# An MLP that streams its weights from HBM: seven raw buffers instead of five, transfers issued ten chunks ahead, and the kept banks of the last block fetched in two parts

## The chip, the cores and the metric

The kernel runs on one core of one Trainium2 chip, in a single launch. The metric is the device time in microseconds (us), lower is better. The kernel before the change was timed three times; the numbers below give the median and the spread.

## The reference, cut to what matters

A decoder trunk of two layers on one sequence of 256 tokens, 2048 features, all in float32. Each layer is an attention mixer, an MLP and a gated per-layer embedding (called PLE below). The change lies in the MLP and touches the start of the PLE that follows it:

```python
for i in range(DEPTH):                               # DEPTH = 2, D_MODEL = 2048, D_FF = 8192, SEQ = 256
    ...                                              # attention mixer A (layer 0) or B (layer 1)
    hn = rmsnorm(h, mlp_norm_g[i])
    h = h + jnp.square(jax.nn.relu(hn @ mlp_w1[i])) @ mlp_w2[i]
    gate = jax.nn.sigmoid(rmsnorm(h, ple_norm_g[i]) @ ple_w_gate[i])
    h = h + (p[i] @ ple_w_proj[i]) * gate
return rmsnorm(h, final_norm_g)
```

## The kernel before, in words

**Chunks.** Every weight is read once, in chunks of 128 partitions x 1024 float32 (512 KB). A chunk passes through four stations. SP issues its DMA into a tile `raw` (L262, queue order is program order). ACT copies it to a rounded tile `whi` (L274). DVE subtracts and so makes the remainder `wlo` (L282). TensorE then forms three products for each pair of operands, high x high, low x high and high x low, each with 512 columns (L525 in the pair scheme below, L636 in the plain scheme). There are 5 `raw`, 6 `whi` and 5 `wlo` buffers. A `raw` buffer is free again when its `wlo` has been made.

**The order of the work.** All instructions are laid down by `Program.run` (L144), which walks through the list of chunks. At the step of chunk `at` it first issues loads up to chunk `at + 7` (DMA_AHEAD), stopping earlier when the `raw` buffer that comes next in turn has not yet had its `wlo` laid down; then copies and subtractions up to about three chunks ahead (SPLIT_AHEAD); then every running generator is advanced by one `yield` (this is how evacuations, transposes, norms and other side work are spread over the steps); then come the matmuls of chunk `at`. So a generator's place in the order is counted in chunk steps, and each engine and each DMA queue works through its part of that order without overtaking.

**The MLP.** `mlp` (L790) runs over four blocks of the hidden width (NFB = 4, `b`), each with four groups of up products (`q`) and four of down products. Pairs of groups are made with a seven-product scheme (`pair_major`, L492): a chunk step is of kind `q` (plain, 12 matmuls) or one of `a`, `b`, `t`, `u`, where `t` and `u` are sums of raw chunks that DVE makes (L564, L569, L570) and have no load of their own; the raw tiles of `a` and `b` are held until `u`'s `wlo`. The sums over the blocks are kept in DRAM: for `b < 3`, `down_kept` (L967) adds each block's banks to DRAM tiles `s` (four 128x512 halves, in two tiles for each pair of groups) and `y` by accumulating DMAs on the POOL queue (L896). The hidden activations are transposed through DRAM on the POOL queue as well (L225, L229).

**The last block.** For `b = 3` the pair of groups 0 and 1 is made by `down_last` (L986), the groups 2 and 3 by the plain scheme. `fetch_shared(0)` (L944) reads the kept `s` tiles of the first pair into tiles `xf`. When the seven-product sums of the last block are there, `sums` adds them (L992), joins them (`from_sums`, L932 to L935) and issues on POOL, in this order: two accumulating DMAs that add `y[0]` and `y[1]` (L997), the fetch of the second pair's two `s` tiles (L944), and the fetch of `y[2]` and `y[3]` (L948). Each is 512 KB. `finish_sums(2)` is started behind them; after three `yield`s it joins the second pair's sums on DVE, and later adds `y[2]` and `y[3]` (`with_y`, L951). The first pair's result is finished by `done` (L1010), transposed on DVE (L761), sent through DRAM on the SP queue (`dU`, written at L225 and read back at L229) and added to the residual `x` (L778); then come the squares and the normed copies for the PLE (L379, L303 on ACT, L385, L311 on DVE). The groups 2 and 3 follow the same way (L906). The PLE's first chunks are loaded while this goes on, and one small product with the sum of squares `acc` (L320) closes the norm.

**Pools.** Tiles that live only during the MLP are in a pool `z`. It is opened 12 chunks into the MLP and closed after the last down chunk. `raw`, `whi` and `wlo` are in a pool of the whole program.

Of the kernel before, what the change touches and what calls it, by code (L numbers as in the profile page):

```python
# [10 lines left out]
F32 = mybir.dt.float32  # L11
# [4 lines left out]
P = 128  # L16
# [12 lines left out]
NFB = 4  # L29
CH = 1024  # L30
# [3 lines left out]
DMA_AHEAD = 7  # L34
SPLIT_AHEAD = 3
RAW_BUFS, HI_BUFS, LO_BUFS = 5, 6, 5
HF_BUFS = 3
FORM_LATER = (7, 9)
MIXED = (2, 3, 5, 6)
MIXED_QK = (5, 6, 7)  # L40
# [19 lines left out]
def f32(ap):  # L60
    return ap.bitcast(F32)
# [13 lines left out]
class Part:  # L75
# [3 lines left out]
    def __init__(self, src=None, make=None, cols=None, held=0):  # L79
        self.src, self.make, self.cols, self.held = src, make, cols, held  # L80
# [9 lines left out]
class Program:  # L90
# [7 lines left out]

    def __init__(self):
        self.steps, self.active, self.waiting, self.after = [], [], [], []  # L100

    def op(self, fn):
        self.steps.append((None, fn))

    def chunk(self, src, fn):
        self.steps.append((src if isinstance(src, Part) else Part(src), fn))

    def collect(self, fn):
        kept, self.steps = self.steps, []
# [31 lines left out]
        except StopIteration:  # L141
            pass

    def run(self, load, copy, sub):  # L144
        srcs = [s for s, _ in self.steps if s is not None]
        raw, hi, lo = {}, {}, {}
        held = []
        loaded = at = copied = subbed = 0
        for src, fn in self.steps:
            if src is None:  # L150
                g = fn()
                if g is not None:
                    self.begin(g)
                continue
            starting = at < KT // 2
            if starting:
                self.advance()
            urgent = [g.gen for g in self.waiting if isinstance(g, Urgent)]
            self.waiting = [g for g in self.waiting if not isinstance(g, Urgent)]
            for g in urgent:  # L160
                next(g)
            ahead = max(0, min(SPLIT_AHEAD, at - KT // 2 + 2))
            while loaded < len(srcs) and loaded <= at + DMA_AHEAD:
                if srcs[loaded].make is None:
                    if len(held) >= RAW_BUFS and held[-RAW_BUFS] >= subbed:
                        break
                    raw[loaded] = load(loaded, srcs[loaded].src)
                    held.append(loaded + srcs[loaded].held)
                loaded += 1
            while copied < loaded and copied <= at + ahead + (ahead > 0):  # L170
                if srcs[copied].make is not None:
                    raw[copied] = srcs[copied].make(raw, copied)
                hi[copied] = copy(copied, raw[copied], srcs[copied].cols)
                copied += 1
            while subbed < copied and subbed <= at + ahead:
                lo[subbed] = sub(subbed, raw[subbed], hi[subbed], srcs[subbed].cols)
                subbed += 1
            for n in [n for n in raw if n + srcs[n].held < subbed]:
                del raw[n]
            if not starting:  # L180
                self.advance()
            self.active += urgent
            self.waiting += fn(hi.pop(at), lo.pop(at)) or []
            self.finish_tensor()
            at += 1
        self.until(lambda: not self.active and not self.waiting)
# [3 lines left out]
def kernel(ctx: ExitStack, tc: tile.TileContext, a: dict, out: bass.AP):  # L190
    nc = tc.nc
    ctx.enter_context(tc.manual_schedule())
    prog = Program()
# [6 lines left out]
    wpool = ctx.enter_context(tc.tile_pool(name="w", bufs=4))  # L200
# [3 lines left out]
    cur = {}  # L204
# [6 lines left out]
    def close_pool(key):  # L211
        cur.pop(key)
        cur.pop(key + "/es").close()
# [41 lines left out]
    def load_x(j, order="xTA"):  # L255
        nc.sync.dma_start(xp[j], a[order][:, j * 2 * T:(j + 1) * 2 * T])


    def load(n, src):
        t = wpool.tile([P, CH], F32, tag="raw", name="raw", bufs=RAW_BUFS)  # L260
        for c in pieces(n) if n == 0 else [slice(0, CH)]:
            nc.sync.dma_start(t[:, c], src[:, c])  # L262
        if n < KT // 2 - 1:
            load_x(n + 1)
        return t

    def pieces(n):

        return [slice(0, CH // 2), slice(CH // 2, CH)] if n < 2 else [slice(0, CH)]
# [520 lines left out]
    def mlp(layer, xg, norm, to, norm2, opening):  # L790
# [3 lines left out]

        y = [dpool.tile([P, D // 2], F32, tag=f"y{q}", name=f"y{q}", bufs=1) for q in range(4)]
        shared = {q: [dpool.tile([P, D // 2], F32, tag=f"s{q}{i}", name=f"s{q}{i}", bufs=1) for i in range(2)] for q in (0, 2)}
        hid = [[None] * 16 for _ in range(NFB)]
# [18 lines left out]
        def up(b, q, t, late=0):  # L818
# [19 lines left out]
            for n in range(2 if third_group(b, q) else 1):  # L838
                if n:
                    for _ in range(FORM_LATER[b > 0]):  # L840
                        yield
# [6 lines left out]
                yield  # L848
                f = cur["z"].tile([P, 2, 2 * T], F32R, tag="hf", name="hf", bufs=HF_BUFS)
                f5 = f.rearrange("p c (i a r) -> p c a i r", i=4, r=32)  # L850
# [65 lines left out]
        def chunks(w, b, q):  # L916
            return lambda c: a[w][layer * 128 + (b * 4 + q) * 8 + c]
# [4 lines left out]
        def downs(b, q):  # L922
            token_major(chunks("w2", b, q), hid[b], lambda *ps: down(b, q, *ps), whole=True)

        def all_forms(these):
            for c in these:
                yield from x_forms(2 * c, G_MLP + layer, forms)
                yield
# [10 lines left out]
        def fetch_shared(q):  # L939

            kept[q] = [cur["z"].tile([P, 2, 2 * T], F32R, tag="xf", name="xf", bufs=len(MIXED)) for _ in range(2)]
            kept[q] = [f32(t) for t in kept[q]]
            for i in range(2):
                nc.gpsimd.dma_start(kept[q][i], shared[q][i])  # L944
# [8 lines left out]
            merged.add(q + i)  # L953

        def finish_sums(q):
            for _ in range(3):
                yield
            from_sums(*kept[q])
            for i in range(2):
                for _ in range(2):  # L960
                    yield
                with_y(q, i)

        def turning_tile(n):
            return f32(cur["z"].tile([P, 2, 2 * T], F32R, tag="hf", name="hf", bufs=HF_BUFS).rearrange("p c n -> p (c n)"))

# [19 lines left out]
        def down_last(q):  # L986
            ts = []

            def sums(aux):
                for t, names in zip(kept[q], (("P1", "R6"), ("Q5", "Q7"))):  # L990
                    for j, n in enumerate(names):
                        nc.vector.tensor_add(t[:, j], aux[n], t[:, j])  # L992
                    yield
                from_sums(*kept[q])
                yield
                for i in range(2):
                    nc.gpsimd.dma_start(kept[q][i], y[q + i], accum_op=ALU.add)  # L997
                fetch_shared(2)
                fetch(2)
                fetch(3)  # L1000
                prog.waiting.append(finish_sums(2))
                for _ in range(4):
                    yield
                ts.extend(kept[q])

            def done(i, ps):
                while not ts:
                    yield
                t = ts[i]
                nc.vector.tensor_add(t, ps, t)  # L1010
                yield
                w = yield from turned(t, turning_tile if i else new, steps=3)
                add_turned(q + i, w)
                yield
                yield from in_pairs(normed, q + i)

            return sums, done

        def down_mixed(b, q):
            sums, done = down_kept(b, q) if b < NFB - 1 else down_last(q)  # L1020
            m = mixed_down(b, q)
            if (b, q) == (0, 0):
                order = [(i, c) for i in range(2) for c in (1, 2, 3)] + [(0,)] + [(i, c) for c in (4, 5) for i in range(2)]
            else:
                order = [(0, c) for c in (1, 2, 3)] + [(0,)] + [(1, c) for c in (1, 2, 3)]
                order += [(4,)] if third_group(b, q) else [(0, 5), (1, 5), (4,)]
            if third_group(b, q):
                order += [(0, 6), (1, 6), (5,), (0, 7), (1, 7)]
            else:
                order += [(i, c) for i in range(2) for c in (6, 7)]  # L1030
            pair_major(lambda i, c: a["w2"][layer * 128 + (b * 4 + q + i) * 8 + c], order, hid[b], turned_forms[b], sums, done,
                       {(0, 0): {13: [lambda: all_forms(MIXED[3:])]}, (NFB - 1, 0): {1: [lambda: fetch_shared(0)]}}.get((b, q)), (3, 1, 0, 2), urgent=b < NFB - 1)

        up_mixed(0, 2)
        for b in range(NFB):
# [4 lines left out]
                up_mixed(b + 1, 2)  # L1040
        downs(NFB - 1, 2)
        downs(NFB - 1, 3)
        prog.op(lambda: close_pool("z"))
        prog.op(lambda: open_pool("j"))
        prog.op(lambda: open_pool("R", side="right"))
# [945 lines left out]
    prog.op(lambda: open_pool("E"))  # L1991
    ple(1, p1, x_p1, n_p1, None, n_fin, True)

    prog.run(load, copy, sub)
    close_pool("E")
    close_pool("j")
    close_pool("h")
# [121 lines left out]
```

## Time and profile before

| | |
|---|---|
| median of 3 runs | 2407.78 us (2405.53 to 2411.17) |
| the profiled execution | 2413.49 us, of which the instructions span 2411.7 us |
| TensorE busy | 2392.0 us, 11159 matmuls |
| DVE busy | 2059.4 us |
| ACT busy | 1519.9 us |
| DMA queue of SP | 508.37 MB, 65.7% of 16 engines' span |
| DMA queue of POOL | 68.19 MB, 10.9% |

The profile is of one execution. Its lines name an engine, a line of the kernel and tiles (`out<-in`); a bracket behind a timeline row gives the idle time of the engine before that row and what ended it. PE is TensorE's matmul, PEld its weight load. A PE that shows as busy need not run at its full rate, so lost time is better read from the number of matmuls in a stretch. Times in rows are counted from the first instruction. In this execution the MLP of layer 0 takes its pair-scheme products from 507 us and ends near 1133 us; that of layer 1 runs from 1670 us to near 2300 us; the last blocks begin near 1047 and 2210 us.

### The profile page before, as it was taken

How to read it: one execution, taken by the hardware profiler on the slowest of the kernel's cores; microseconds unless marked ns; L12 is line 12 of the kernel's file. 1: busy time of each engine (PE TensorE's matmuls, PEld its weight loads, DVE VectorE, ACT ScalarE, POOL GpSimd, SP SyncE). 2: the span in 40 equal slices, each digit the busy share in tenths (PEclk: the TensorE clock that was granted, in tenths of full speed). 3: DMA queues.
4: the chain of work that ended last, by engine and by line, in shares of the span. 5: the costliest groups of instructions: out<-in, count | busy, mean ns of one | idle time of the engine just before them, and what ended most of it. 6: DMA issues, size and time to landing. Idle time of an engine off the chain costs nothing.

```text
span 2411.7 us, 32754 instructions
## 1 busy us (share of the span) xinstructions
PE 2392.0 (99%) x11159; PEld 1993.6 (83%) x11159; DVE 2059.4 (85%) x2926; ACT 1519.9 (63%) x2211; POOL 144.6 (6%) x246
## 2 busy tenths in 40 slices
PE   9999999999999999999999999999999999999998
PEld 8888888888888888877788889988888888888777
DVE  7978886788999999897777989867999899898886
ACT  7555555666666656664564788756666666666466
POOL 0000000001001100111000000000100100111000
PEclk9999999999999999999999999999999999999999
DMA  8778678778778788889887853477868878878984
GB/s 287 238 233 264 222 246 284 233 220 269 236 258 257 247 259 253 252 264 283 252 241 205 266 158 123 136 231 220 281 216 259 262 250 244 258 246 274 267 269 148
DMA packets 181289, 579.44 MB, mean 240 GB/s; under 512 B 21633, under 2 KB 44161, under 8 KB 181121
## 3 DMA queue, kind: packets, MB, share of 16 engines
q1 hardware_dynamic: 160080, 508.37, 65.7%
q0 software_dynamic: 20464, 68.19, 10.9%
q8 instruction: 87, 1.43, 0.2%
q10 hardware_dynamic: 576, 0.79, 0.1%
q14 instruction: 82, 0.66, 0.1%
HBM read 511.21 MB, written 66.06 MB: 239 GB/s over the span
## 4 chain that ended last, share of the span: by engine, by line
PE 89%; DMA 4%; DVE 3%; issue 2%; ACT 1%; SPq 0%; POOL 0%; DVEq 0%; ACTq 0%; POOLq 0%
PE at L525 42%; PE at L636 15%; PE mm L525 10%; PE mm L636 10%; PE mm L415 4%; PE mm L417 2%; DVE wlo L282 1%; PE at L415 1%; DMA dU<-z 1%; DMA w<-dU 1%; DMA xf<-s 1%; PE at L417 1%; DMA raw<-in_w_proj 1%; PE at L1941 1%; DMA raw<-in_w 0%
## 5 line engine op out<-in xcount | busy, mean ns | idle before, releaser
L282 DVE TENSOR_TENSOR wlo<-raw,whi 128x1024 fp32r<-128x1024 f32 (+1 forms) x973 | 1103.2, 1161 | 205.0 <-ACT whi L274 67.7
L274 ACT CAST whi<-raw 128x1024 fp32r<-128x1024 f32 (+1 forms) x973 | 946.1, 1005 | 422.9 <-DMA raw<-in_w 117.1
L525 PE MATMUL at<-whi,xa 128*128 128x512 f32 x1512 | 465.9, 389 | 0.0
L525 PE MATMUL at<-whi,h 128*128 128x512 f32 x1408 | 433.5, 389 | 0.0
L525 PEld LDWEIGHTS at<-whi,xa 128*128 128x128 f32 x1512 | 283.7, 188 | 59.4
L525 PEld LDWEIGHTS at<-whi,h 128*128 128x128 f32 x1408 | 264.3, 188 | 54.7
L525 PE MATMUL at<-wlo,xa 128*128 128x512 f32 x756 | 294.2, 389 | 0.0
L636 PE MATMUL at<-whi,xa 128*128 128x512 f32 x928 | 287.4, 391 | 0.1
L525 PE MATMUL at<-wlo,h 128*128 128x512 f32 x704 | 274.3, 390 | 0.8 <-DVE wlo L282 0.8
L274 ACT CAST whi<-ts 128x1024 fp32r<-128x1024 f32 x98 | 103.3, 1054 | 186.8 <-DVE ts L564 149.1
L636 PE MATMUL mm<-whi,xa 128*128 128x512 f32 x656 | 204.1, 392 | 0.0
L636 PEld LDWEIGHTS at<-whi,xa 128*128 128x128 f32 x928 | 172.6, 188 | 36.1 <-ACT whi L274 0.8
L636 PE MATMUL at<-wlo,xa 128*128 128x512 f32 x464 | 180.9, 391 | 0.6 <-DVE wlo L282 0.6
L525 PEld LDWEIGHTS at<-wlo,xa 128*128 128x128 f32 x756 | 141.9, 188 | 29.6
L525 PEld LDWEIGHTS at<-wlo,h 128*128 128x128 f32 x704 | 132.1, 188 | 29.7 <-DVE wlo L282 2.4
L636 PEld LDWEIGHTS mm<-whi,xa 128*128 128x128 f32 x656 | 123.2, 189 | 25.0
L636 PE MATMUL mm<-wlo,xa 128*128 128x512 f32 x328 | 128.4, 391 | 2.3 <-DVE wlo L282 2.3
L564 DVE TENSOR_TENSOR ts<-raw 128x1024 f32<-128x1024 f32 x98 | 119.3, 1217 | 5.7 <-DMA raw<-in_w 4.6
L282 DVE TENSOR_TENSOR wlo<-ts,whi 128x1024 fp32r<-128x1024 f32 x98 | 119.4, 1219 | 2.5 <-PE at L636 1.6
L415 PE MATMUL mm<-xa,whi 128*128 128x512 f32 x336 | 109.8, 399 | 0.0
L636 PEld LDWEIGHTS at<-wlo,xa 128*128 128x128 f32 x464 | 87.1, 188 | 20.6 <-DVE wlo L282 2.3
L525 PE MATMUL mm<-whi,xf 128*128 128x512 f32 x324 | 99.9, 390 | 0.0
(443 smaller groups left out, 3487.3 us busy)
## 6 DMA issues: line engine op xcount, KB each, us to landing
raw<-in_w SPq DMA_DIRECT2D x512, 512.0 KB, 4.9
raw<-in_w_qk SPq DMA_DIRECT2D x96, 512.0 KB, 5.0
raw<-in_w_gate SPq DMA_DIRECT2D x64, 512.0 KB, 4.9
raw<-in_w_kv SPq DMA_DIRECT2D x48, 512.0 KB, 4.4
raw<-in_w_v SPq DMA_DIRECT2D x47, 512.0 KB, 5.3
raw<-in_w_q SPq DMA_DIRECT2D x32, 512.0 KB, 4.2
raw<-in_w_oB SPq DMA_DIRECT2D x32, 512.0 KB, 3.8
dU<-z POOLq DMA_DIRECT2D x30, 512.0 KB, 4.6
```

What stands on the lines that cost most here:

```text
L274: nc.scalar.copy(hi[:, c], t[:, c])
L282: nc.vector.tensor_sub(lo[:, c], t[:, c], f32(hi)[:, c])
L415: nc.tensor.matmul(ps, hi[:, col:col + P], rhs, start=first, stop=False)
L417: nc.tensor.matmul(ps[:, :T], lo[:, col:col + P], rhs[:, :T], start=False, stop=last)
L525: nc.tensor.matmul(ps, x_, w_, start=b not in touched, stop=end and last[b] == n and i == 2)
L564: nc.vector.tensor_add(halves(t), halves(a), b[:, None, :512].to_broadcast([P, 2, 512]))
L636: nc.tensor.matmul(st[j], *parts[j][i], start=k == i == 0, stop=k == kt - 1 and i == 2)
L1941: nc.tensor.transpose(tr[:, i * P:(i + 1) * P], src, ident)
```

## The change

It has two parts.

Seven raw buffers: while the MLP's chunks are loaded and `z` is open, loads go in turn to the five `raw` buffers and to two new buffers `rawx` in `z`, and the limit on how far ahead loads are issued goes from 7 to 10 chunks. The load that comes next still waits until the buffer it takes has had its `wlo` laid down. Chunks of other stages keep five buffers and the limit of 7.

The fetch in two parts: in the last block the fetch of the second pair's `s` tiles is taken out of `sums` and put behind step 14 of the pair's 20 steps (counted from 0), ahead of the accumulating DMAs; `finish_sums(2)` is started behind step 15. It now waits six `yield`s ahead of `from_sums`, then three and two ahead of the two `with_y`. The fetch of `y[2]` and `y[3]` stays where it was.

```diff
+RAW_MORE, MORE_AHEAD = 2, 3
...
     def chunk(self, src, fn):
-        self.steps.append((src if isinstance(src, Part) else Part(src), fn))
+        part = src if isinstance(src, Part) else Part(src)
+        part.deep = self.deep
+        self.steps.append((part, fn))
...
-        held = []
+        held, turn = {"raw": [], "more": []}, 0
...
-            while loaded < len(srcs) and loaded <= at + DMA_AHEAD:
+            while loaded < len(srcs):
+                more = srcs[loaded].deep and roomy()
+                if loaded > at + DMA_AHEAD + (MORE_AHEAD if more else 0):
+                    break
                 if srcs[loaded].make is None:
-                    if len(held) >= RAW_BUFS and held[-RAW_BUFS] >= subbed:
+                    turn = (turn + 1) % (RAW_BUFS + RAW_MORE) if more else 0
+                    tag, bufs = ("more", RAW_MORE) if turn > RAW_BUFS else ("raw", RAW_BUFS)
+                    if more and turn == 0:
+                        tag, bufs = "more", RAW_MORE
+                    if len(held[tag]) >= bufs and held[tag][-bufs] >= subbed:
+                        turn -= 1
                         break
-                    raw[loaded] = load(loaded, srcs[loaded].src)
-                    held.append(loaded + srcs[loaded].held)
+                    raw[loaded] = load(loaded, srcs[loaded].src, tag == "more")
+                    held[tag].append(loaded + srcs[loaded].held)
                 loaded += 1
...
-    def load(n, src):
-        t = wpool.tile([P, CH], F32, tag="raw", name="raw", bufs=RAW_BUFS)
+    def load(n, src, more=False):
+        t = cur["z"].tile([P, CH], F32, tag="rawx", name="rawx", bufs=RAW_MORE) if more else \
+            wpool.tile([P, CH], F32, tag="raw", name="raw", bufs=RAW_BUFS)
...
         def finish_sums(q):
-            for _ in range(3):
+            for _ in range(6):
                 yield
             from_sums(*kept[q])
             for i in range(2):
-                for _ in range(2):
+                for _ in range(3 - i):
                     yield
                 with_y(q, i)
...
                     nc.gpsimd.dma_start(kept[q][i], y[q + i], accum_op=ALU.add)
-                fetch_shared(2)
                 fetch(2)
                 fetch(3)
-                prog.waiting.append(finish_sums(2))
...
-                       {(0, 0): {13: [lambda: all_forms(MIXED[3:])]}, (NFB - 1, 0): {1: [lambda: fetch_shared(0)]}}.get((b, q)), (3, 1, 0, 2), urgent=b < NFB - 1)
+                       {(0, 0): {13: [lambda: all_forms(MIXED[3:])]}, (NFB - 1, 0): {1: [lambda: fetch_shared(0)], 
+                                         14: [lambda: fetch_shared(2)],
+                                         15: [lambda: finish_sums(2)]}}.get((b, q)), (3, 1, 0, 2), urgent=b < NFB - 1)
...
-    prog.run(load, copy, sub)
+    prog.run(load, copy, sub, lambda: "z" in cur)
```

More of the change, by code (lines that the diff above doesn't have):

```diff
@@ L100, in __init__ @@
         self.steps, self.active, self.waiting, self.after = [], [], [], []
+        self.deep = False
     def op(self, fn):
@@ L142, in begin, with run @@
             pass
-    def run(self, load, copy, sub):
+    def run(self, load, copy, sub, roomy):
         srcs = [s for s, _ in self.steps if s is not None]
         raw, hi, lo = {}, {}, {}
-        held = []
+        held, turn = {"raw": [], "more": []}, 0
         loaded = at = copied = subbed = 0
@@ L790, in mlp @@
     def mlp(layer, xg, norm, to, norm2, opening):
+        prog.deep = True
         y = [dpool.tile([P, D // 2], F32, tag=f"y{q}", name=f"y{q}", bufs=1) for q in range(4)]
@@ L1042, in mlp @@
         downs(NFB - 1, 3)
+        prog.deep = False
         prog.op(lambda: close_pool("z"))
```

## The prediction

> **What bounds the kernel now.** I read the page first, then the stretches table, then who ends TensorE's waits, then the timelines of DVE, ACT, POOL and SP around the last block of the MLP.
>
> ```profile
> PE 2392.0 (99%) x11159; PEld 1993.6 (83%) x11159; DVE 2059.4 (85%) x2926; ACT 1519.9 (63%) x2211; POOL 144.6 (6%) x246
> PE 89%; DMA 4%; DVE 3%; issue 2%; ACT 1%; SPq 0%; POOL 0%; DVEq 0%; ACTq 0%; POOLq 0%
> ```
>
> TensorE is busy for 99% of the span and carries 89% of the chain. The change takes no matmul away, so all it can win is time in which TensorE waits. The stretches table (stretch, length, then busy time and count of each engine, granted clock, DMA share, GB/s) says how much that is:
>
> ```profile
> 507.00:858.00 351.00, 351.00 (x1550) 290.66 (x1549) 322.80 (x366) 228.94 (x270) 38.86 (x66) 1.00 0.81 253
> 858.00:1047.00 189.00, 187.96 (x825) 153.97 (x824) 173.32 (x186) 121.03 (x139) 18.13 (x28) 1.00 0.82 251
> 1047.00:1135.00 88.00, 86.78 (x379) 70.59 (x378) 72.29 (x80) 42.62 (x50) 13.13 (x24) 1.00 0.91 283
> 1135.00:1167.00 32.00, 30.14 (x132) 24.28 (x132) 26.43 (x44) 23.35 (x43) 5.45 (x10) 1.00 0.82 255
> 1167.00:1180.00 13.00, 11.43 (x46) 9.07 (x45) 9.03 (x15) 5.87 (x8) 0.00 (x0) 0.87 0.77 252
> 2020.00:2210.00 190.00, 189.30 (x832) 155.46 (x831) 175.36 (x188) 122.64 (x141) 18.12 (x28) 1.00 0.82 250
> 2210.00:2300.00 90.00, 88.66 (x389) 72.53 (x388) 74.58 (x86) 44.90 (x56) 10.59 (x18) 1.00 0.93 281
> 2300.00:2329.00 29.00, 28.13 (x123) 22.60 (x122) 24.45 (x39) 21.43 (x36) 0.00 (x0) 1.00 0.79 263
> ```
>
> In 507 to 858 us TensorE never waits: 351.00 / 1550 = 0.2265 us per matmul. At that pace 825 matmuls take 186.8 us, so 858 to 1047 loses 2.2 us. In the same way 1047 to 1135 (last block, layer 0) loses 88 - 85.8 = 2.2, 1135 to 1167 (start of the PLE) 32 - 29.9 = 2.1; in layer 1, 2020 to 2210 loses 190 - 188.4 = 1.6, 2210 to 2300 loses 90 - 88.1 = 1.9, and 2300 to 2329 loses 29 - 27.9 = 1.1. The sum is 11.1 us. The stretch from 1167 holds 42 large matmuls (9.5 us) and four with one column, taken as 0.3 us together, so 3.2 us are lost there to something else: the last product of the norm (L320).
>
> What ends these waits, in the table of waits for TensorE's weight loads from 1047 to 1180 us (total, times, longest):
>
> ```profile
> PEld mm L636 <- DVE wlo L282: 2.8, 2, 2.1
> PEld at L636 <- DVE wlo L282: 2.0, 3, 0.8
> PEld mm L320 <- DVE acc L311: 2.0, 1, 2.0
> PEld at L525 <- DVE wlo L282: 0.8, 1, 0.8
> ```
>
> Each time it is a `wlo` that DVE made late. Why DVE was late differs by stretch, and so does what the edit can do.
>
> **Part A, two more raw buffers in the body of the MLP (2.2 + 1.6 us).** The largest wait of 858 to 1047, in the timeline of DVE and of the weight loads:
>
> ```profile
> 1022.00 1.23 DVE L564 TENSOR_TENSOR ts<-raw 128x1024 f32<-128x1024 f32 x1 [1.38 <-DMA raw<-in_w]
> 1026.35 0.19 PEld L525 LDWEIGHTS mm<-wlo,xf 128*128 128x128 f32 x1 [1.03 <-DVE wlo L282]
> ```
>
> DVE stands 1.38 us for a raw chunk, and 4 us later TensorE stands for the `wlo` made of it. A plain chunk feeds 12 matmuls, 12 x 0.2265 = 2.7 us, so two more buffers let a load start up to 2 x 2.7 = 5.4 us earlier, far more than waits of about 1 us need. Issue order allows it: at step `at` the `wlo`s of chunks up to `at + 2` are laid down, so with five buffers loads reach `at + 7` and with seven `at + 9`; either way the last one waits on `wlo(at + 2)`, so SP stands no longer than now. The wire has room to get ahead: 251 GB/s here against 283 in 1047 to 1135, so at 32 GB/s to spare the 1.05 MB of two chunks are gained in 33 us. Copies and subtractions keep their order, so ACT and DVE are asked for nothing new. Bounds: 0 (the two chunks never get ahead) to 3.8; I take 3.8, since the row says that a chunk was late.
>
> **Part B, the last block (2.2 + 1.9 us).** The timelines of POOL, ACT and DVE in layer 0:
>
> ```profile
> 1066.76 2.18 POOL L229 DMA_DIRECT2D y<-dU  x4 [5.70 <-DMA dU<-z]
> 1089.02 1.85 POOL L997 DMA_DIRECT2D xf<-y  x2 [20.09 <-DVE xf L934]
> 1090.32 1.66 POOL L944 DMA_DIRECT2D xf<-s  x2
> 1091.61 1.42 POOL L948 DMA_DIRECT2D y<-y  x2
> ```
> ```profile
> 1100.77 1.05 ACT L274 CAST whi<-raw 128x1024 fp32r<-128x1024 f32 x1 [6.74 <-DMA raw<-in_w]
> 1103.33 1.05 ACT L274 CAST whi<-raw 128x1024 fp32r<-128x1024 f32 x1 [1.52 <-DMA raw<-in_w]
> 1105.89 1.05 ACT L274 CAST whi<-raw 128x1024 fp32r<-128x1024 f32 x1 [1.50 <-DMA raw<-in_w]
> ```
> ```profile
> 1097.11 1.22 DVE L1010 TENSOR_TENSOR xf<-at,xf 128x1024 f32<-128x1024 f32 x1
> 1103.08 0.69 DVE L932 TENSOR_TENSOR xf<-xf 128x512 f32<-128x512 f32 x1 [4.75 <-DMA xf<-s]
> 1105.71 0.69 DVE L933 TENSOR_TENSOR xf<-xf 128x512 f32<-128x512 f32 x1 [1.94 <-DMA xf<-s]
> 1107.77 1.22 DVE L1010 TENSOR_TENSOR xf<-at,xf 128x1024 f32<-128x1024 f32 x1
> 1110.04 1.24 DVE L761 STREAM_TRANSPOSE z<-xf 128x1024 f32<-128x1024 f32 x1
> ```
>
> Six POOL transfers of 512 KB start together at 1089. Two accumulate; then raw chunks come in every 2.56 us, and the `s` tiles, between them, 2.63 us apart. ACT stands 6.74 us for raw data. DVE stands 4.75 + 1.94 = 6.7 us at `from_sums(2)`, and behind it in DVE's order wait the second `done`, every later `wlo` and the transposes.
>
> Count steps of the last block from its first down chunk: the plain chunks of groups 2 and 3 are 20 to 27 and 28 to 35, the PLE begins at 36. Before, `sums` ran at 16 to 19 and `from_sums(2)` at 23. After, `finish_sums(2)` runs once behind step 15 and six advances later joins at 21; `with_y` goes from 25 and 27 to 24 and 26.
>
> The fetch of `s`, put behind step 14, comes in POOL's order after the transposes of the hidden tiles (last issue 1066.8 to 1068.9) and ahead of the wait for L934, so near 1069, 20 us before its use. Its two `xf` tiles are free, since the up products that read them ended by 1047. What it adds near 1069 is 1 MB beside the raw loads, two turns of 2.56 us; the 5.4 us of part A cover that, and without them up to 5.1 us of raw delay per layer would reach TensorE.
>
> At 1089 four transfers are left. `y[2]` and `y[3]` take the places of the `s` tiles, landing near 1103.1 and 1105.7. So what is late next is the second accumulation (at 1103.1 less 2.6 = 1100.5) for `done`, and `y[2]` at 1103.1 for `with_y` at step 24. On DVE: L1010 ends at 1098.3, waits 2.2 us, runs 1.2, then a `wlo` of 1.2 ends at 1102.9, then 0.2 us for `y[2]`. The waits fall from 6.7 to 2.4 us, and with `with_y` ahead of them the transposes start near 1104.3 instead of 1110.0. The `wlo` that TensorE lacked at 1110 is then 7 us early. Four L932-type instructions (4 x 0.69 = 2.8 us) move two steps up, between `wlo`s that have that slack. Bounds: 0 (the waits move to `y`) to 4.1; I take 4.1.
>
> **Part C, the start of the PLE (2.1 + 1.1 us).** The timelines of SP and DVE:
>
> ```profile
> 1113.53 3.73 SPq L262 DMA_DIRECT2D raw<-in_w  x3
> 1117.57 1.75 SPq L229 DMA_DIRECT2D w<-dU  x4
> 1119.43 4.59 SPq L229 DMA_DIRECT2D hf<-dU  x4
> ```
> ```profile
> 1126.27 1.29 DVE L778 TENSOR_TENSOR x<-w,x 128x512 f32<-128x512 f32 x2 [1.35 <-DMA w<-dU]
> 1130.60 1.29 DVE L778 TENSOR_TENSOR x<-hf,x 128x512 f32<-128x512 f32 x2 [3.04 <-DMA hf<-dU]
> 1131.82 2.35 DVE L282 TENSOR_TENSOR wlo<-raw,whi 128x1024 fp32r<-128x1024 f32 x2
> 1161.92 1.29 DVE L778 TENSOR_TENSOR x<-w,x 128x512 f32<-128x512 f32 x2 [5.57 <-DMA w<-dU]
> ```
>
> DVE stands 1.35 + 3.04 = 4.4 us for the first pair's transposed rows, and behind them wait the last `wlo` of the MLP and all the norm's work. After, the transposes start 5.7 us earlier, and three raw loads that stand between `dU`'s write and its read on SP (1113.53 to 1117.26) are laid down ahead of the write, since loads run two chunks further ahead. So the rows land at least 5.7 us earlier and the 4.4 us of standing go; DVE reaches the PLE that much ahead, which covers the 2.1 us lost from 1135 to 1167, and likewise the 1.1 of layer 1. The queue behind: the loads of the PLE keep the old limit and come on SP after the reads, as now.
>
> I leave the last product's 3.2 us where they are: `acc` hangs on the round trip of group 3 through DRAM (`x<-w` at 1161.92 after 5.57 us of standing), which no edit shortens. Bounds of C: 0 to 3.2 plus that 3.2 and layer 1's 0.9 (below). I take 3.2.
>
> One price sits in that last term:
>
> ```profile
> 1170.00:1173.40 3.40, 3.40 (x10) 2.72 (x11) 3.02 (x4) 1.07 (x2) 0.00 (x0) 0.50 0.76 241
> 1169.60 0.66 PE L320 MATMUL mm<-ones,acc 128*128 128x1 f32 x4 [1.57 <-DVE acc L311]
> PEld mm L320 <- DVE acc L311: 0.9, 1, 0.9
> ```
>
> (The last row is that of 2210 to 2345.) Right after a gap of 1.57 us the granted clock is 0.50 for 3.4 us: about 1.5 us of the 3.2. [...]
>
> **Sum.** 3.8 + 4.1 + 3.2 = 11.1 us off the profiled 2413.5 gives 2402.4. That execution was 5.7 us above the median of the runs, 2407.8, from which the same 11.1 gives 2396.7 us. About 0.2% (4.8 us) is what a measurement of this kernel tells from no change.
>
> **The rivals.**
> Everything goes (0.17): once DVE is ahead, the last product no longer waits either: another 3.2 + 0.9 = 4.1 us, 2392.6. For it, DVE's standing in C is longer than what TensorE loses; against it, the 5.57 us of round trip.
> The waits move (0.15): in the last block the wire is 0.91 to 0.93 busy; raw loads get only every other turn however many are queued, the prefetch is drained there, and DVE stands for `y` instead of `s`. Only A is won: 2404.0. [...]
> The depth does little (0.10): `a`, `b` and the load-free `t`, `u` hold buffers so long that the body's late chunks stay late; B and C come from the split fetch alone: 3.8 less, 2400.5.
> Slower (0.08): SP is in order, and with seven buffers two more raw loads can be on the wire ahead of `dU`'s write. At 2.56 us each that is 5.1 us on the chain transposes, rows, norm, last product, in both layers. It decides where TensorE already waits for that chain, at 1167 and 2329; then B and C are given back there, and 3.8 - 10.2 = 6.4 us are lost: 2414.2. Against it: by then the MLP's loads have been issued for steps, not queued up.
>
> **How the numbers follow.** The forecast has 0.50; its own range is 2393.5 to 2400. The range 2391.5 to 2404.5 takes in all but the slower case and the edges. Faster by over 0.2% (below 2403.0): nearly all of the forecast, everything goes, most of the third rival, and some of the second, 0.76. Within 0.2%: most of the second and the rest, 0.16. Slower: 0.08.
>
> **What would show it.** A: no `PEld ... <- DVE wlo` at L525 in the body of either MLP, matmuls at 0.2265 us from 858 to 1047. B: `xf<-s` in POOL's rows near 1069, L932 without a wait, the transposes about 6 us nearer to the accumulation. C: L778 of the first pair with no standing. Wrong would be: raw waits on ACT as long as now, a new wait at L951 above 2 us, or a longer wait at L320.

## The result and the profile after

| | before | after |
|---|---|---|
| median | 2407.65 us (2405.53 to 2411.80, 6 runs) | 2395.22 us (2395.08 to 2396.37, 6 runs) |
| profiled execution | 2413.49 us, span 2411.7 us | 2395.12 us, span 2393.3 us |

The ratio is 0.9947, with a 95% interval of 0.9934 to 0.9960: 12.4 us less. The runs of after also lie closer together, 1.3 us from end to end where those of before take 6.3 us. Two single slow runs are left out of the medians and ranges below, 2976.45 us of the kernel with six buffers and the old fetch and 6226.73 us of the one without the later blocks' writes.

In after, lines of the kernel stand 13 lower in its first part and 14 or 15 lower in the last (L282 is L295, L636 is L649, L320 is L333, L932 is L946, L997 is L1011). The page's row of busy times and its row of the chain:

```profile
PE 2383.0 (100%) x11159; PEld 1993.3 (83%) x11159; DVE 2057.9 (86%) x2926; ACT 1517.7 (63%) x2211; POOL 144.4 (6%) x246
PE 99%; DMA 0%; ACT 0%; DVE 0%; SPq 0%; issue 0%; ACTq 0%; DVEq 0%
```

The chain is now 99% TensorE where it was 89%, and DMA, DVE and ACT have all but left it. The stretches table (start and end, length, then busy time and count of PE, PEld, DVE, ACT, POOL, granted clock, DMA share, GB/s), for the stretches of the prediction:

```profile
858.00:1047.00 189.00, 189.00 (x836) 156.49 (x835) 175.64 (x189) 120.65 (x140) 19.78 (x31) 1.00 0.83 256
1047.00:1135.00 88.00, 88.00 (x390) 72.88 (x389) 79.90 (x101) 52.74 (x70) 16.80 (x31) 1.00 0.91 293
1135.00:1167.00 32.00, 32.00 (x145) 26.58 (x144) 22.24 (x33) 16.86 (x23) 0.00 (x0) 1.00 0.77 239
2020.00:2210.00 190.00, 190.00 (x840) 157.34 (x839) 175.43 (x189) 123.01 (x143) 22.53 (x36) 1.00 0.86 261
2210.00:2300.00 90.00, 90.00 (x399) 74.53 (x398) 78.91 (x99) 50.65 (x68) 6.16 (x10) 1.00 0.90 285
2300.00:2329.00 29.00, 29.00 (x132) 24.05 (x131) 18.88 (x29) 16.28 (x23) 0.00 (x0) 1.00 0.70 215
```

The first column after the length says it: TensorE is busy for the whole of each stretch, and 88 us now hold 390 matmuls where they held 379. 88 / 390 = 0.2256 and 189 / 836 = 0.2261 us each (one matmul more or less at an edge is 0.23 us), the pace that 507 to 858 us always had. (In 1135 to 1167 four of the 145 have one column.) From 1047 to 1180 us the table of waits for TensorE's weight loads has no row left.

The last block, in the timelines of POOL and DVE:

```profile
1062.89 1.10 POOL L958 DMA_DIRECT2D xf<-s  x2
1084.67 1.85 POOL L1011 DMA_DIRECT2D xf<-y  x2 [20.68 <-DVE xf L948]
```
```profile
1088.42 0.68 DVE L946 TENSOR_TENSOR xf<-xf 128x512 f32<-128x512 f32 x1
...
1097.26 1.23 DVE L965 TENSOR_TENSOR xf<-xf,y 128x1024 f32<-128x1024 f32 x1 [0.21 <-DMA y<-y]
1098.41 1.24 DVE L774 STREAM_TRANSPOSE z<-xf 128x1024 f32<-128x1024 f32 x1
...
1115.17 1.29 DVE L791 TENSOR_TENSOR x<-w,x 128x512 f32<-128x512 f32 x2
...
1136.00 1.24 DVE L774 STREAM_TRANSPOSE z<-xf 128x1024 f32<-128x1024 f32 x1
...
1146.93 1.29 DVE L791 TENSOR_TENSOR x<-w,x 128x512 f32<-128x512 f32 x2 [1.75 <-DMA w<-dU]
...
1154.39 0.41 DVE L324 TENSOR_TENSOR acc<-acc,sq 128x256 f32<-128x256 f32 x1
```

The `s` tiles are fetched at 1062.9, and 25 us later L946 adds them without a wait; from the sums to the transposes DVE stands 0.21 us, where it stood 6.7. The first pair's transposed rows are taken at 1115.17 with no standing. ACT, which stood 6.74 us for raw data at this place, is now held back by TensorE, which frees the `whi` buffers:

```profile
1100.15 1.06 ACT L287 CAST whi<-raw 128x1024 fp32r<-128x1024 f32 x1 [1.67 <-PE mm L649]
```

The norm's last product, which no part of the forecast sum touched, in TensorE's timeline:

```profile
1160.02 0.50 PE L333 MATMUL mm<-ones,acc 128*128 128x1 f32 x4
```

It follows the matmul before it without a gap. Its `acc` was ready at 1154.39 + 0.41 = 1154.80, 5.2 us before.

How far the same matmul starts earlier in after than in before, from the two traces, which hold the same 11159 matmuls in the same order (the gain per row is what that piece of the program gave):

| near, in after | earlier by | gained since the row above | what lies between |
|---|---|---|---|
| 860 us | 0.82 us | 0.82 | all before the body; 0.44 of it ahead of the MLP |
| 1034 | 2.99 | 2.17 | body of the MLP, layer 0 |
| 1133 | 5.39 | 2.40 | last block |
| 1152 | 7.85 | 2.46 | start of the PLE |
| 1173 | 11.34 | 3.49 | norm's last product, and the clock behind it |
| 2197 | 13.21 | 1.87 | to the end of layer 1's body |
| 2276 | 15.35 | 2.14 | last block, layer 1 |
| 2312 | 16.85 | 1.50 | start of the PLE |
| 2330 | 17.64 | 0.79 | norm's last product |
| 2385 | 18.37 | 0.73 | the rest |

### The profile page after: what moved, and what is told of

It is laid out like the page before. It is cut to its first block, busy times and chain, and to the rows that moved or that the text cites. A ratio compares the mean times of both kernels' runs of the same rounds, so it can differ in the third digit from the quotient of the medians.

```text
span 2393.3 us, 32751 instructions
## 1 busy us (share of the span) xinstructions
PE 2383.0 (100%) x11159; PEld 1993.3 (83%) x11159; DVE 2057.9 (86%) x2926; ACT 1517.7 (63%) x2211; POOL 144.4 (6%) x246
## 4 chain that ended last, share of the span: by engine, by line
PE 99%; DMA 0%; ACT 0%; DVE 0%; SPq 0%; issue 0%; ACTq 0%; DVEq 0%
PE at L538 44%; PE at L649 17%; PE mm L649 13%; PE mm L538 11%; PE mm L428 4%; PE mm L430 2%; PE at L428 1%; PE at L430 1%; PE at L1956 1%; PE mm L1980 0%; PE mm L1719 0%; PE mm L1720 0%; PE mm L1137 0%; PE mm L1139 0%; DMA raw<-in_w_v 0%; PE mm L1138 0%
## 5 line engine op out<-in xcount | busy, mean ns | idle before, releaser
L295 DVE TENSOR_TENSOR wlo<-raw,whi 128x1024 fp32r<-128x1024 f32 (+1 forms) x813 | 930.9, 1167 | 199.8 <-PE at L649 49.6
L287 ACT CAST whi<-raw 128x1024 fp32r<-128x1024 f32 (+1 forms) x813 | 800.7, 1011 | 311.3 <-PE mm L649 78.8
L538 PE MATMUL at<-whi,xa 128*128 128x512 f32 x1512 | 465.7, 389 | 0.0
L538 PE MATMUL at<-whi,h 128*128 128x512 f32 x1408 | 433.4, 389 | 0.0
L538 PEld LDWEIGHTS at<-whi,xa 128*128 128x128 f32 x1512 | 283.7, 188 | 59.2
L538 PEld LDWEIGHTS at<-whi,h 128*128 128x128 f32 x1408 | 264.2, 188 | 54.8
L538 PE MATMUL at<-wlo,xa 128*128 128x512 f32 x756 | 294.2, 389 | 0.0
L649 PE MATMUL at<-whi,xa 128*128 128x512 f32 x928 | 287.0, 391 | 0.4 <-ACT whi L287 0.4
L538 PE MATMUL at<-wlo,h 128*128 128x512 f32 x704 | 273.9, 389 | 0.0
L649 PE MATMUL mm<-whi,xa 128*128 128x512 f32 x656 | 202.8, 390 | 0.0
L649 PEld LDWEIGHTS at<-whi,xa 128*128 128x128 f32 x928 | 172.2, 188 | 36.6 <-ACT whi L287 1.3
L295 DVE TENSOR_TENSOR wlo<-rawx,whi 128x1024 fp32r<-128x1024 f32 (+1 forms) x160 | 177.6, 1130 | 15.8 <-ACT whi L287 13.4
L649 PE MATMUL at<-wlo,xa 128*128 128x512 f32 x464 | 180.7, 390 | 0.5 <-DVE wlo L295 0.5
L287 ACT CAST whi<-rawx 128x1024 fp32r<-128x1024 f32 (+1 forms) x160 | 152.7, 979 | 32.5 <-DVE rawx L583 14.0
L538 PEld LDWEIGHTS at<-wlo,xa 128*128 128x128 f32 x756 | 141.9, 188 | 29.6
L538 PEld LDWEIGHTS at<-wlo,h 128*128 128x128 f32 x704 | 132.1, 188 | 27.5
L649 PEld LDWEIGHTS mm<-whi,xa 128*128 128x128 f32 x656 | 122.4, 188 | 24.9
L649 PE MATMUL mm<-wlo,xa 128*128 128x512 f32 x328 | 127.7, 389 | 0.0
L295 DVE TENSOR_TENSOR wlo<-ts,whi 128x1024 fp32r<-128x1024 f32 x98 | 119.4, 1219 | 6.9 <-ACT whi L287 5.3
L649 PEld LDWEIGHTS at<-wlo,xa 128*128 128x128 f32 x464 | 87.0, 188 | 19.8 <-DVE wlo L295 1.7
```

Of the source, the lines that this page charges most:

```text
L287: nc.scalar.copy(hi[:, c], t[:, c])
L295: nc.vector.tensor_sub(lo[:, c], t[:, c], f32(hi)[:, c])
L538: nc.tensor.matmul(ps, x_, w_, start=b not in touched, stop=end and last[b] == n and i == 2)
L649: nc.tensor.matmul(st[j], *parts[j][i], start=k == i == 0, stop=k == kt - 1 and i == 2)
```

## The experiments

My theory after the result: the two halves of the edit do different work. The buffers take the waits out of the body (A); the fetch in two parts takes them out of the last block and the PLE (B, C, and with them the norm's product). The rival: the buffers alone do everything, since a `wlo` is late only where raw data is late.

### Each half alone

Buffers alone, against the kernel after:

```diff
-            for _ in range(6):
+            for _ in range(3):
...
-                for _ in range(3 - i):
+                for _ in range(2):
...
+                fetch_shared(2)
                 fetch(2)
                 fetch(3)
+                prog.waiting.append(finish_sums(2))
...
-                                         14: [lambda: fetch_shared(2)],
-                                         15: [lambda: finish_sums(2)]}}.get((b, q)), (3, 1, 0, 2), urgent=b < NFB - 1)
```

> Seven buffers and the limit of ten chunks alone; the fetch of the last block as before. My theory: the body of the MLP loses nothing (3.8 us won, part A), but the join of the second pair's sums still stands about 6.7 us for the s tiles on DVE, the wlo behind it stays late, and TensorE's waits in the last block, at the start of the PLE and at the norm's last product stay: about 2404 us. Rival, the buffers do it all (DVE was late only because raw chunks were late): no wait of TensorE left, about 2395 us.

Measured: 2395.86 us (2395.53 to 2396.11), 0.9949 [0.9937, 0.9961] of before (2407.90, timed beside it). The rival is right about the time; its reason does not hold everywhere, as the kernel with seven buffers in the last block alone shows below. The stretch of the last block, DVE's timeline, ACT's row for the same chunk and the norm's product:

```profile
1047.00:1135.00 88.00, 88.00 (x390) 72.93 (x389) 76.34 (x93) 48.84 (x65) 16.85 (x31) 1.00 0.91 285
```
```profile
1098.05 0.69 DVE L946 TENSOR_TENSOR xf<-xf 128x512 f32<-128x512 f32 x1 [2.76 <-DMA xf<-s]
1100.69 0.69 DVE L947 TENSOR_TENSOR xf<-xf 128x512 f32<-128x512 f32 x1 [1.95 <-DMA xf<-s]
...
1159.23 0.42 DVE L324 TENSOR_TENSOR acc<-acc,sq 128x256 f32<-128x256 f32 x1
```
```profile
1100.80 1.06 ACT L287 CAST whi<-raw 128x1024 fp32r<-128x1024 f32 x1 [1.66 <-PE mm L649]
```
```profile
1160.67 0.50 PE L333 MATMUL mm<-ones,acc 128*128 128x1 f32 x4
```

DVE still stands 2.76 + 1.95 = 4.7 us for the `s` tiles, yet TensorE has no gap: 390 matmuls in 88 us, as in after. With raw chunks on the chip ACT's copies keep TensorE's pace through the same congestion, and DVE's 4.7 us are covered: I take it that `wlo`s made ahead pay for them. The margin is thinner than in after: `acc` is ready at 1159.65, 1.0 us before its product, not 5.2.

The split fetch alone, against the kernel after (five buffers, limit 7):

```diff
-        prog.deep = True
```

> The fetch in two parts alone, five buffers and the limit of seven. My theory: the waits of the body stay (3.8 us), those of the last block, the PLE's start and the norm's last product go: about 2399 us. Rival, the buffers do it all: about 2407 us, since 3 MB less 1 MB still drain five buffers at the accumulation, and the 1 MB now comes at a moment when raw chunks are late already.

Measured: 2400.83 us (2400.19 to 2402.84), 0.9969 [0.9958, 0.9981]. Two stretches, then all waits of the weight loads from 1047 to 1180, and POOL's row of the early fetch:

```profile
858.00:1047.00 189.00, 188.76 (x830) 155.26 (x829) 173.46 (x186) 120.84 (x138) 18.15 (x28) 1.00 0.81 251
1047.00:1135.00 88.00, 86.51 (x379) 70.50 (x378) 78.71 (x94) 49.01 (x62) 13.11 (x24) 1.00 0.95 299
```
```profile
1059.28 0.19 PEld L538 LDWEIGHTS mm<-wlo,hf 128*128 128x128 f32 x1 [0.67 <-DVE wlo L295]
1061.54 0.19 PEld L538 LDWEIGHTS at<-wlo,h 128*128 128x128 f32 x1 [1.03 <-DVE wlo L295]
1079.60 0.50 PEld L538 LDWEIGHTS at<-whi,h 128*128 128x128 f32 x2 [0.28 <-ACT whi L287]
1081.05 0.19 PEld L538 LDWEIGHTS at<-wlo,h 128*128 128x128 f32 x1 [0.95 <-DVE wlo L295]
```
```profile
1069.27 1.10 POOL L957 DMA_DIRECT2D xf<-s  x2
```

The waits at L649 at the end of the block and in the PLE, and that at the norm's product, are gone, as the theory had it; those of the body stay. But layer 0's last block holds 379 matmuls in 88 us, as before: 2.9 us of waits at L538, which lay at 0.8 us before. The first two, 1.7 us, come ahead of the early fetch, and the second execution of before (below) has 0.18 and 1.04 us at the same two chunks. The last two, 1.2 us, come 10 us behind the fetch. They could be the price that the prediction put at up to 5.1 us if part A's cover were missing, but that is not shown: the kernel with seven buffers in the last block alone (below) keeps the old fetch and has 0.97 and 0.95 us at the same two places.

The two halves win 12.0 and 7.1 us, and together 12.4, not 19: both remove the same waits at the end of the last block, in the PLE and at the norm.

### What of the buffers, and what of the fetch

The limit of ten chunks taken back, the buffers kept:

```diff
-RAW_MORE, MORE_AHEAD = 2, 3
+RAW_MORE, MORE_AHEAD = 2, 0
```

> The changed kernel with seven buffers, but loads issued only seven chunks ahead. My theory: in plain stretches a load at step at+7 takes the buffer of chunk at, which has long been free, so a load is issued as late in program order as before, yet it no longer waits for wlo(at+2) on SP; issue in time is then bounded by SP reaching it, so part of A is kept: 2396 to 2399 us. Rival, the limit is idle and only the number of buffers counts: 2395 us, no wait in the body. Rival, the limit is all: body as before, 2399 us.

Measured: 2395.49 us (2394.98 to 2395.79), 0.9948 [0.9936, 0.9960]. The limit does nothing here; the number of buffers is what ends the loads.

The early fetch kept, but the joins put back to their old place:

```diff
-            for _ in range(6):
+            for _ in range(3):
...
-                for _ in range(3 - i):
+                for _ in range(2):
...
+                prog.waiting.append(finish_sums(2))
...
-                                         14: [lambda: fetch_shared(2)],
-                                         15: [lambda: finish_sums(2)]}}.get((b, q)), (3, 1, 0, 2), urgent=b < NFB - 1)
+                                         14: [lambda: fetch_shared(2)]}}.get((b, q)), (3, 1, 0, 2), urgent=b < NFB - 1)
```

> The changed kernel with the s tiles fetched early but joined at the old place (step 23 instead of 21, y added at 25 and 27). My theory: what stood was the transfer, so the join no longer stands, the four joins of 0.69 us lie ahead of the second done and put the transposes 3 us later than after the change, which the slack of DVE covers: 2395 to 2396 us. Rival, the place of the join is what counts (the transposes behind it): 2397 us or more, with a wait at the norm's last product.

Measured: 2395.71 us (2395.41 to 2396.84), 0.9950 [0.9938, 0.9962]: where the joins stand does not show.

### How many buffers, and where

One buffer more instead of two, with the old fetch (the edit of the buffers alone, and this line), and then with the split fetch (this line alone):

```diff
-RAW_MORE, MORE_AHEAD = 2, 3
+RAW_MORE, MORE_AHEAD = 1, 2
```

> Six raw buffers instead of seven, the fetch of the last block as before. The run with seven buffers alone came out where the changed kernel is, so the theory now is that any slack in raw chunks is enough once it exceeds the waits, which were under 2 us each; one buffer is worth 2.7 us. Expected: 2396 to 2398 us, no wait in the bodies, perhaps a few tenths at the norm's last product, whose acc came 1.0 us early with seven buffers. Rival, two chunks are needed, since the burst of the last block keeps raw chunks away for 9 us: half of the gain, about 2401 us, with waits in the last blocks.

> Six raw buffers and the fetch in two parts. Theory that slack adds up: no wait left, 2395.2 to 2396 us, as with seven. Rival, the early fetch costs raw chunks near step 8 of the last block, as it did with five buffers (0.4 to 0.9 us at three places there): 2396.5 us or more with waits there.

Measured: 2396.43 us (2395.81 to 2400.25), 0.9944 [0.9926, 0.9962] with the old fetch, and 2395.39 us (2395.12 to 2396.34), 0.9937 [0.9923, 0.9951] with the split (before, timed beside them, was 2409.78). The sixth buffer wins all but what cannot be told apart; in the profile of the first no wait is left in either MLP.

Seven buffers for the last block's chunks alone, old fetch (the edit of the buffers alone, and this):

```diff
-        prog.deep = True
...
         for b in range(NFB):
+            prog.deep = b == NFB - 1
```

> Seven buffers for the chunks of the last block alone, five in the body of the MLP, the fetch as before. Theory that the gains are local: the body's waits stay (3.8 us in the profile of before), all later ones go: 2398 to 2400 us. Rival, what the last block needs is a lead gathered in the body: its waits come back, 2402 us or more.

Measured: 2404.78 us (2399.03 to 2406.88, 12 runs), 0.9977 [0.9967, 0.9987]. Most of the gain is lost, as the rival had it, but not for its reason alone. The last blocks of layers 0 and 1, then ACT and DVE in that of layer 0 and the first wait of the weight loads behind them:

```profile
1047.00:1135.00 88.00, 85.97 (x374) 69.59 (x374) 74.88 (x88) 45.48 (x59) 13.14 (x24) 1.00 0.91 284
2210.00:2300.00 90.00, 90.00 (x399) 74.53 (x398) 80.30 (x101) 52.78 (x71) 8.97 (x15) 1.00 0.89 288
```
```profile
1106.88 1.06 ACT L287 CAST whi<-rawx 128x1024 fp32r<-128x1024 f32 x1 [1.67 <-PE mm L649]
```
```profile
1103.24 0.69 DVE L945 TENSOR_TENSOR xf<-xf 128x512 f32<-128x512 f32 x1 [4.60 <-DMA xf<-s]
1105.87 0.69 DVE L946 TENSOR_TENSOR xf<-xf 128x512 f32<-128x512 f32 x1 [1.94 <-DMA xf<-s]
```
```profile
1110.34 0.19 PEld L649 LDWEIGHTS mm<-wlo,h 128*128 128x128 f32 x1 [0.51 <-DVE wlo L295]
```

In layer 0 the block holds 374 matmuls, even fewer than before's 379; in layer 1 it holds 399, as in after. Raw chunks are not what is missing at the block's end: from 1085 to 1115 us each copy on ACT that waits does so for TensorE, as in the row. But DVE stands 4.60 + 1.94 = 6.5 us for the `s` tiles, the `wlo`s behind that come late, and TensorE waits 0.51 us here and 0.80 us at 1113.73. So DVE's standing for `s` can cost time by itself: 4.7 us of it cost nothing with the buffers throughout, 6.5 us cost 1.3 us here. The block's other waits, 2.7 us, lie between 1059 and 1081 us; ahead of the last two of them ACT stood 3.81 us for a transposed hidden tile (`y<-dU`), not for a raw chunk. The bodies, with five buffers, also lose time of their own: 830 and 828 matmuls, where after has 836 and 840. Why the last block of layer 1 got by in this execution is open.

### Before once more

The prediction took its terms from one execution of before, which was 5.7 us over the median. One more, unchanged:

> The kernel before, unchanged, for a second profile. Theory: the executions of before differ by how long TensorE waits in the MLPs, and the profiled one, 5.7 us above the median, had more of it: with a time nearer to 2407 us the waits in the same stretches add up to about 12 us instead of 18. Rival: the waits are the same and the 5.7 us lie elsewhere.

It took 2401.76 us (span 2400.0 us). The same stretches and the norm's product; the granted clock right behind that, from 1166 to 1169 us, was 1.00:

```profile
858.00:1047.00 189.00, 189.00 (x832) 155.60 (x831) 174.29 (x187) 122.31 (x141) 18.13 (x28) 1.00 0.81 251
1047.00:1135.00 88.00, 86.75 (x380) 70.68 (x379) 74.31 (x87) 44.35 (x57) 14.91 (x29) 1.00 0.92 290
1135.00:1167.00 32.00, 30.43 (x134) 24.28 (x133) 26.84 (x42) 23.00 (x37) 3.68 (x6) 1.00 0.80 267
2020.00:2210.00 190.00, 190.00 (x838) 156.59 (x837) 176.22 (x190) 122.84 (x141) 20.01 (x32) 1.00 0.83 255
2210.00:2300.00 90.00, 90.00 (x398) 74.37 (x397) 78.12 (x98) 51.05 (x70) 8.69 (x15) 1.00 0.91 287
```
```profile
1165.22 0.60 PE L320 MATMUL mm<-ones,acc 128*128 128x1 f32 x4 [1.13 <-DVE acc L311]
```

By the prediction's pace of 0.2265 us the five stretches lose 0.6, 1.9, 2.3, 0.2 and nothing, 5.0 us, and that includes the norm's product, which falls into the third here (130 large matmuls and four of one column at 0.3 us). In the first profile the same places lost 2.2 + 2.2 + 2.1 + 1.6 + 1.9 + 3.2 = 13.2 us. The difference, 8.2 us, makes up most of the 11.7 us between the two spans. So these two executions of before differ mostly by the very waits that the change removes; for the others it is not shown.

### Why raw chunks came late in the body

The blocks after the first add their kept sums to DRAM with an accumulating transfer. Theory: those transfers hold up the raw loads. First plain writes in their place (the same bytes; the sums over the blocks are not formed), then no writes but the first block's:

```diff
-            nc.gpsimd.dma_start(to, flat(t), **({"accum_op": ALU.add} if b else {}))
+            nc.gpsimd.dma_start(to, flat(t))
```

> The kernel before (five buffers) with the accumulation of the kept sums left out: each block writes s and y without adding, the same bytes on the same queue, so the sums over the blocks are not formed. Theory that raw chunks are late in the body because the accumulating transfers keep the wire (landing 8.4 and 13.5 us after issue against 4.6 and 6.3 us for the first block's plain writes): the waits where seven-product chunks follow them (near 859, 1025 and 2188 us) go, those at the start of a down group (912, 1060) and of the last block stay, 2 to 3 us less than the kernel before. Rival, any 2 MB of POOL traffic delays raw chunks as much: as the kernel before.

```diff
-            nc.gpsimd.dma_start(to, flat(t), **({"accum_op": ALU.add} if b else {}))
+            if b == 0:
+                nc.gpsimd.dma_start(to, flat(t))
```

> The kernel before with the kept sums written by the first block alone, so the second and third block's share is left out of the result and 4 MB of POOL traffic of each block is not moved. Theory: as with plain writes, the waits near 859, 1025 and 2188 us are gone; if plain writes keep them and this one does not, it is the traffic and not the adding. Rival, raw chunks are late for want of buffers whatever POOL moves: the waits stay in all.

Measured: 2400.22 us (2397.37 to 2406.66), 0.9966 [0.9953, 0.9979] with plain writes, and 2405.56 us (2403.21 to 2408.36), 0.9984 [0.9975, 0.9993] without those of the later blocks (before, timed beside them, was 2408.84). The body of both layers with plain writes:

```profile
858.00:1047.00 189.00, 189.00 (x835) 156.55 (x834) 174.60 (x187) 121.57 (x140) 16.66 (x31) 1.00 0.77 254
2020.00:2210.00 190.00, 190.00 (x840) 157.38 (x839) 175.46 (x188) 125.38 (x144) 19.18 (x35) 1.00 0.80 259
```

No time is lost there, with five buffers: more than I expected, since two waits that I thought independent of the writes went as well. Waits at L636 and at the norm's product stay, which is why the buffers win more. This is one profile; the second execution of before lost only 0.6 and 0.2 us in its two bodies, so what the accumulation costs there varies. The DMA view from 1000 to 1030 us, first of before, then with plain writes (`q0` is POOL's queue: packets, MB, share of the 16 DMA engines' time; then issues, KB each, median us to landing):

```profile
q0 software_dynamic: 576, 2.10, 37.3%
...
raw<-in_w SPq DMA_DIRECT2D x11, 512.0 KB, 7.5
s<-y POOLq DMA_DIRECT2D x2, 512.0 KB, 8.4
y<-y POOLq DMA_DIRECT2D x2, 512.0 KB, 13.5
```
```profile
q0 software_dynamic: 576, 2.10, 18.7%
...
raw<-in_w SPq DMA_DIRECT2D x10, 512.0 KB, 4.4
s<-y POOLq DMA_DIRECT2D x2, 512.0 KB, 6.3
y<-y POOLq DMA_DIRECT2D x2, 512.0 KB, 6.9
```

With accumulation the same 2.10 MB take twice the share of the DMA engines' time, a transfer of 512 KB takes up to twice as long to land, and the raw loads beside it land after a median of 7.5 us, not 4.4. (In two other windows with such transfers the raw loads differ less: 5.2 us against 4.8 from 830 to 880 us, and 4.9 us from 2155 to 2200 us against 4.6 from 2150 to 2200 with plain writes.) Without the later blocks' writes the body is free too (836 matmuls from 858 to 1047), but the last block is worse, not better. Raw chunks come late in it, ACT standing 4.18 us for one at 1095.64; why they do is open:

```profile
1047.00:1135.00 88.00, 85.31 (x374) 69.63 (x373) 69.48 (x79) 40.11 (x47) 12.64 (x24) 1.00 0.90 277
```

## Why the prediction was right, and where it was wrong

The forecast was 2396.7 us, the median came out at 2395.22 us, 1.5 us lower and inside the range. The mechanism held: in the stretches that the forecast named, each wait of TensorE for a late `wlo` is gone. Behind the total, four steps were off.

**A, the body: right.** 2.2 us in layer 0 (forecast 2.2), and in layer 1 no wait is left. Buffers do it: the split alone leaves 830 matmuls in the stretch. What made raw chunks late, which the prediction left unnamed, is the accumulating writes, as far as single profiles show it: without accumulation no wait is left in either body, with five buffers. The estimate that the lead takes some 33 us to gather was not tested: the kernel that had the buffers in the last block alone won 5.0 us where six buffers throughout won 13 to 14, but its waits there were not for raw chunks alone.

**B and C: right in size, wrong in the shares.** 2.4 and 2.1 us came from the last blocks (forecast 2.2 and 1.9), 2.5 and 1.5 us from the starts of the PLE (forecast 2.1 and 1.1). The prediction gave B to the split fetch, on the ground that DVE's standing for `s` is what TensorE waits for. The ground holds: the split alone takes away the waits at the block's end, and with the buffers in the last block alone a standing of 6.5 us cost 1.3 us. What failed is that only the split could help: the buffers alone win the same, since the standing falls from 6.7 to 4.7 us and no longer reaches TensorE. The rival "the depth does little" is out, and so is "the waits move": the wire in the last block is still 0.91 busy, but the prefetch was not drained: from 1084 to 1106 us ACT stands 1.66 or 1.67 us ahead of each copy, never for raw data. Raw loads did get about every other turn while both queues moved data: SP's moved 0.41 MB and POOL's 0.42 from 1100 to 1102 us in before, 0.43 and 0.41 from 1094 to 1096 us in after. That this holds however many are queued was not shown. In the working of B, the wait for `y[2]` was put at 0.2 us and measured 0.21; the 2.2 us for the second accumulation did not come, so the transposes follow the accumulation's issue by 1098.41 - 1084.67 = 13.7 us, not 21.0: 7.3 us nearer, where I said about 6.

**The norm's last product: wrong.** The step that failed is "`acc` hangs on the round trip of group 3 through DRAM, which no edit shortens", for which 3.2 and 0.9 us were kept. The rows show that the round trip was not what decided. In before it starts at this row of DVE:

```profile
1149.47 1.24 DVE L761 STREAM_TRANSPOSE z<-xf 128x1024 f32<-128x1024 f32 x1
```

From there to `x<-w` it took 1161.92 - 1149.47 = 12.5 us, in after 1146.93 - 1136.00 = 10.9. It starts 13.5 us earlier, since DVE no longer comes to it late from the last block (in before it worked without a pause from 1131.82 us up to there). Against TensorE: in before it reached the product at 1169.60 - 1.57 = 1168.03, 18.6 us behind that row, while `acc` took 20.1 us from there; in after `acc` took 18.8 us and had 24.0. A round trip that starts earlier ends earlier: I looked at its length and not at its start. The table of shifts gives 3.5 and 0.8 us for the two products. The rival "everything goes" had this, at 0.17.

**The clock: not settled.** The half clock, about 1.5 us, went with the gap: the clock is 1.00 from 1167 to 1180 us in after. The second execution of before had a gap of 1.13 us at the same product, and the clock stayed at 1.00, so this term was not even in every execution. The length of the gap alone does not decide it either. In the kernel without the later blocks' writes TensorE stood longer, at this product in layer 1, and the clock was 1.00 from 2326 to 2345 us:

```profile
2325.40 0.61 PE L320 MATMUL mm<-ones,acc 128*128 128x1 f32 x4 [1.76 <-DVE acc L311]
```

The 1.57 us gap of the first profile had 0.50 after it. After has no such gap, so these runs do not settle what halved the clock.

**The base: wrong, and it hid the former.** I took 11.1 us, read in an execution 5.7 us above the median, off the median. With the norm's 4.1 us the waits of that execution were 15.2 us; it got 18.4 us faster, the rest being pieces of at most 0.8 us, some of them ahead of the MLP. Off its own 2413.5, 11.1 us would have given 2402.4. But between the medians there were only 12.4 us to win. A term too many in the base and a term too few in the sum nearly cancelled, and that the forecast came within 1.5 us is in part luck; "everything goes" off the median came to 2392.6, 2.6 us too low, for the same reason.

**SP's queue.** The rival of a slower kernel had two more raws ahead of `dU`'s write. SP's timeline in after:

```profile
1099.67 0.33 SPq L237 DMA_DIRECT2D dU<-z  x1
...
1101.90 0.33 SPq L275 DMA_DIRECT2D rawx<-in_w  x1
1105.18 1.75 SPq L241 DMA_DIRECT2D w<-dU  x4
```

One raw load stands between write and read, where three did (I said none), and the read is issued 5.5 us after the write. In before it was 1117.57 - 1111.31 = 6.3 us, so the raw loads in between were worth little: the write itself comes 11.6 us earlier. The read's rows were forecast at least 5.7 us earlier; L791 runs 1126.27 - 1115.17 = 11.1 us earlier.

No kernel tried beats the changed one by more than can be measured: six or seven buffers with or without the split all lie within 2395.2 to 2396.4 us, with TensorE at its pace through both MLPs.

## What to carry to other kernels

Two cures for the same wait do not add: before giving each its share, ask what remains of the wait once the other is in place. A wait that ends a chain is judged by when the chain starts, not only by its own length. Where the runs of a kernel spread, the waits of one profiled execution are not those of the median: subtract them from that execution, or read several.

## What the hardware showed beyond that

From 1000 to 1030 us accumulating transfers to DRAM of 512 KB took 8.4 and 13.5 us to land (medians of two each), where plain writes of the same bytes took 6.3 and 6.9, and the four of them took 37.3% of the DMA engines' time where the plain ones took 18.7%. One TensorE gap of 1.57 us was followed by 3.4 us at half clock; gaps of 1.13 and 1.76 us at the same kind of product were not.
